# Modulation steps put into VectorE's waits, and two sets of matmul operands made 128 rows high

## The chip, the core and the metric

The kernel runs on one core of one Trainium2 chip. The core has TensorE (PE, with its weight loads PEld), VectorE (DVE), ScalarE (ACT), GpSimd (POOL) and SyncE, whose queue (SP) issues nearly all DMAs. Each engine works through its own queue in the order in which the program was built. The metric is the device time of one execution in microseconds (us); lower is better.

## The reference, cut to what matters

One layer over 512 prompt frames and 64 sample frames, width 2048, all float32:

```python
mod = silu(c) @ w_ada + b_ada                    # 2048 x 12288: sh1, sc1, g1, sh2, sc2, g2
h = rmsnorm(x, norm1) * (1 + sc1) + sh1
proj = h @ w_in                                  # a_q a_k a_v a_r a_lr | b_q b_k b_v b_g b_beta b_alpha
log_a = log_sigmoid(a_lr @ gla_wg + gla_bg) / 16 # GLA's forget gate, rank 16
o_a = GLA recurrence (4 heads);  o_b = gated DeltaNet recurrence (8 heads, short conv on q, k, v)
x = x + g1 * (concat(normed, gated o_a, o_b) @ w_out)
h = rmsnorm(x, norm2) * (1 + sc2) + sh2
x = x + g2 * ConvGLU(h; w_up, conv, w_down)
y = rmsnorm(x, final_norm)
```

The "narrow columns" are the 32 columns of `w_in` for a_lr, b_beta and b_alpha. The "mixers" are the two recurrences.

## The kernel before

**TensorE's big products.** Activations are kept transposed, as 16 tiles of 128 rows by 2 x 288 columns (256 prompt frames and 32 sample frames in each half). Each weight is split on the chip into a rounded part `wh` (ScalarE) and the rest `wl` (VectorE), each activation into `hh` and `hl`, and one weight tile of 128 x 128 takes six matmuls of 288 columns (`mm6`, lines 675 and 677): wh with hh, wh with hl, wl with hh, each for two halves. The stages in order of time: a head (norm, the first 4096 modulation columns, six early columns of `w_in`), the mixer stage (the remaining columns of `w_in`, while the mixers run beside them, then half of the product with `w_out`), the rest of `w_out`, the up projection (seven products in place of eight), the down projection and the final norm.

**The mixer stage and its clock.** After each k-tile of the big products (six matmuls) the program builder runs `tick` (line 632). It moves a modelled time `now` by 0.795 us and asks three kinds of generators for their next piece: tasks (short convolutions, the GLA gate), jobs (`gdn`, `gla`: the mixers) and, last, `ada`. Every VectorE, ScalarE and GpSimd operation of these is recorded through `_Timed` (a wrapper; its operations carry line 2297, and line 2272 where they go with a raised priority), which adds a modelled duration to `free[engine]` and to the generator's own `chain`, the modelled time at which its last result is ready. A mixer yields in `until` as long as `now` has not passed its `chain`. So the order in each queue is that in which these generators were asked, and it is fixed when the program is built.

**Modulation steps.** The other 8192 columns of `silu(c) @ w_ada` are computed on VectorE during the mixer stage, in `ada_blocks` (line 1139): 16 blocks of 512 columns, each 16 k-tiles for two conditions (prompt, sample), 512 steps in all. A step is one `scalar_tensor_tensor` of 128 x 512, `acc = w * c + acc`. Four steps use one loaded tile of 512 KB (`aw` or `xr`, two buffers of each; its load is issued on SP at line 1111, three tiles ahead). Behind each 32 steps `ada_sum` adds the partitions with eight matmuls of 32 rows of output (line 1127), and a task puts the sums into `mod`. Credit `at_ada` grows by 0.72 a tick; in `tick` a step is taken while there is credit and VectorE's modelled backlog `free["V"] - now` is under 1.0 us.

**Who waits for VectorE there.** TensorE, for `wl` of the coming weight tiles (three buffers), for `hl` of the mixers' results ahead of the `w_out` product (`load_o`, line 1516, `hl` at 1523), and for results of the mixers' own steps (`m`, `kt`, `rq`, `sl`, `st` in the rows: scratch, row scales and states of the mixers). GpSimd, in the mixers, does the power -1/2 of norms (`rsqrt`) and two `affine_select` masks per DeltaNet head.

**The operands of the second part.** `narrow` (line 1195) copies the 64 used rows of the narrow columns' product into `na` (64 rows, 576 columns), and sorts them by frame with ten matmuls whose other operand is the selector `sel` (lines 1206 and 1208; each float32 matmul is two records in the profile). `gla_gate` (line 1428) multiplies `na` with `wg`, 64 rows of which 32 hold the gate's weights: one matmul of 512 columns and one of 64 for each of four GLA heads.

Of the kernel before, what the change touches and what calls it, by code (L numbers as in the profile page):

```python
# [8 lines left out]
F32 = mybir.dt.float32  # L9
# [7 lines left out]
P = 128  # L17
D = 2048
KD = 16
TP, TS = 512, 64  # L20

HP, HS, HT = 256, 32, 288
# [9 lines left out]

JOB_RATE, ADA_RATE = 1.0, 0.72
TICK_US, HOP_US, DMA_US, ISSUE_US = 0.795, 0.25, 2.6, 0.5
ADA_BACKLOG, ADA_CREDIT = 1.0, 200.0
OP_US = {"V": (0.12, 1 / 960.0), "A": (0.09, 1 / 1060.0), "G": (0.45, 1 / 400.0)}
TABLE_US, COLUMN_US = 1.28, 0.06
TABLES = {AF.Exp: "exp", AF.Silu: "silu", AF.Ln: "ln"}
# [68 lines left out]
WAIT = "wait"  # L107
# [4 lines left out]
class Kern:  # L112
    def __init__(self, tc, ctx, i, o):
        self.tc, self.nc, self.ctx, self.i, self.o = tc, tc.nc, ctx, i, o
        self.n = 0
        self.cp = ctx.enter_context(tc.tile_pool(name="cp", bufs=1, side="left"))
        self.psum = ctx.enter_context(ExitStack())
        self.pg = self.psum.enter_context(tc.tile_pool(name="pg", bufs=2, space=PSUM))
        self.c, self.scrap = {}, []
        self.now, self.chain, self.free = 0.0, None, dict.fromkeys(OP_US, 0.0)  # L120
        self.table, self.floating, self.last_of = None, False, {}
# [510 lines left out]
    def tick(self):  # L632

        self.now += TICK_US
        self.run_due()
        self.run_tasks(list(self.tasks))
        self.at_job += JOB_RATE
        while self.at_job >= 1:
            self.at_job -= 1
            self.job_step()  # L640
        self.at_ada = min(self.at_ada + ADA_RATE, ADA_CREDIT)
        while self.at_ada >= 1 and self.free["V"] - self.now < ADA_BACKLOG:
            r = next(self.ada, self)
            if r is self or r is WAIT:
                break
            self.at_ada -= 1

    def job_step(self):
        for j in list(self.jobs):
# [545 lines left out]
    def narrow(self, pool):  # L1195

        nc, i, c = self.nc, self.i, self.c
        V, A, T = nc.vector, nc.scalar, nc.tensor
        na = self.na = pool.tile([64, TP + TS], F32, name="na")
        V.tensor_copy(na[:, :TP].rearrange("p (h t) -> p h t", h=2), self.ps_nar[:64, :, :HP])  # L1200
        V.tensor_copy(na[:, TP:].rearrange("p (h t) -> p h t", h=2), self.ps_nar[:64, :, HP:HT])
        self.load_consts(None, NARROW)
        g = lambda n, w=36: pool.tile([P, w], F32, name=n)
        ps = self.bank()
        for b in range(4):
            T.matmul(ps[:, b * 16:(b + 1) * 16], na[:, b * P:(b + 1) * P], c["sel"][:64, :16], start=True, stop=True)
        for h in range(2):
            T.matmul(ps[h * 64:(h + 1) * 64, 64:80], na[:, TP:], c["sel"][:64, :16], start=True, stop=True)
        tmp, at = self.m(), [0]

        def g1(w=36):
# [33 lines left out]
        ps = self.bank()  # L1245
# [6 lines left out]
        ps = self.bank()  # L1252
# [15 lines left out]
        ps = self.bank()  # L1268
# [6 lines left out]
        nc.gpsimd.memset(self.wg, 0.0)  # L1275
        nc.sync.dma_start(self.wg[0:16], i["gla_wg"][0])
        nc.sync.dma_start(self.wg[32:48], i["gla_wg"][0])
# [983 lines left out]
class _Sooner:  # L2261
# [5 lines left out]
    def __getattr__(self, name):  # L2267
        f = getattr(self.engine, name)

        def g(*a, **kw):  # L2270
            with self.tc.high_priority(offset=JOB_AHEAD):
                return f(*a, **kw)  # L2272
        return g


def _size(ap):

    n = 1
    for d in ap.shape[1:]:
        n *= d  # L2280
    return n


class _Timed:
# [5 lines left out]
    def __getattr__(self, name):  # L2290
        f = getattr(self.engine, name)

        def g(*a, **kw):
            out = kw["out"] if "out" in kw else a[0]
            self.k.charge(self.key, _size(out), self.k.action(*a[2:], **kw) if name == "activation" else 0.0)
            with self.k.behind(self.key):
                r = f(*a, **kw)  # L2297
# [96 lines left out]
```

## Time and profile before

| what | value |
|---|---|
| time, median of 3 runs | 2743.76 us (2742.51 to 2744.02) |
| the profiled execution's own time | 2741.56 us |
| its span, from first to last instruction | 2739.9 us |
| granted TensorE clock, mean | 0.999 |
| TensorE busy in the span | 2699.0 us (99%) |
| VectorE busy in the span | 2280.0 us (83%) |

A matmul's end in the profile is modelled and matmuls are pipelined, so TensorE counts as busy also where its stream is only slower. What is lost is better seen in three other places: the time between the starts of two matmul rows, the idle time in brackets of a row with what ended it, and the lists of waits (in total, how often, the longest). In a timeline row stand start, duration, engine, line, operation, output<-inputs, shape, and a count where equal rows were merged. Rows of PEld are the weight loads, one ahead of each matmul.

### The profile page before, as it was taken

How to read it: one execution, taken by the hardware profiler on the slowest of the kernel's cores; microseconds unless marked ns; L12 is line 12 of the kernel's file. 1: busy time of each engine (PE TensorE's matmuls, PEld its weight loads, DVE VectorE, ACT ScalarE, POOL GpSimd, SP SyncE). 2: the span in 40 equal slices, each digit the busy share in tenths (PEclk: the TensorE clock that was granted, in tenths of full speed). 3: DMA queues.
4: the chain of work that ended last, by engine and by line, in shares of the span. 5: the costliest groups of instructions: out<-in, count | busy, mean ns of one | idle time of the engine just before them, and what ended most of it. 6: DMA issues, size and time to landing. Idle time of an engine off the chain costs nothing.

```text
span 2739.9 us, 52447 instructions
## 1 busy us (share of the span) xinstructions
PE 2699.0 (99%) x20404; PEld 2632.7 (96%) x20404; DVE 2280.0 (83%) x3691; ACT 1295.7 (47%) x2286; POOL 473.8 (17%) x440
## 2 busy tenths in 40 slices
PE   7999999999999999999999999999999999999998
PEld 5799999999999989999999999999999999999998
DVE  4578887788888898678999999999999976888896
ACT  4245545545644442454545454545454545333453
POOL 0000100001000000001333333333333300000241
PEclk9999999999999999999999999999999999999999
DMA  9985555555565676534464646455655595664762
GB/s 312 344 266 145 152 154 142 148 145 162 168 170 151 177 240 197 148 101 121 138 191 140 188 144 184 149 181 152 179 152 179 151 316 180 209 217 123 238 179 84
DMA packets 645919, 487.61 MB, mean 178 GB/s; under 512 B 66315, under 2 KB 568070, under 8 KB 645670
## 3 DMA queue, kind: packets, MB, share of 16 engines
q1 hardware_dynamic: 632564, 470.77, 57.5%
q10 hardware_dynamic: 13104, 13.47, 1.7%
q8 instruction: 161, 2.64, 0.4%
q14 instruction: 90, 0.72, 0.1%
HBM read 400.12 MB, written 84.04 MB: 177 GB/s over the span
## 4 chain that ended last, share of the span: by engine, by line
PE 89%; DVE 5%; DMA 3%; ACT 1%; issue 1%; SPq 0%; POOL 0%; ACTq 0%; DVEq 0%
PE g L675 19%; PE bank L1785 17%; PE bank L1784 17%; PE bank L1786 17%; PE g L677 9%; PE bank L2316 5%; PE bank L2312 1%; PE bank L675 1%; DVE acc L2297 1%; DVE m L2272 1%; PE bank L904 1%; PE bank L677 1%; DVE wl L1694 0%; DVE wl L2297 0%; PE g L835 0%
## 5 line engine op out<-in xcount | busy, mean ns | idle before, releaser
L1785 PE MATMUL bank<-slot,wh 128*128 128x290 f32 (+1 forms) x3584 | 1067.3, 298 | 0.0
L1784 PE MATMUL bank<-slot,wh 128*128 128x290 f32 (+1 forms) x3584 | 1063.1, 297 | 1.7 <-DVE v L1807 0.6
L1786 PE MATMUL bank<-slot,wl 128*128 128x290 f32 (+1 forms) x3584 | 1060.0, 296 | 1.7 <-DVE wl L1694 1.7
L1786 PEld LDWEIGHTS bank<-slot,wl 128*128 128x128 f32 x3584 | 680.0, 190 | 3.1 <-DVE wl L1694 2.9
L1784 PEld LDWEIGHTS bank<-slot,wh 128*128 128x128 f32 x3584 | 675.4, 188 | 6.3 <-issue 4.7
L1785 PEld LDWEIGHTS bank<-slot,wh 128*128 128x128 f32 x3584 | 676.9, 189 | 0.1
L675 PE MATMUL g<-hh,wh 128*128 128x288 f32 x2048 | 469.5, 310 | 2.2 <-ACT wh L2297 1.3
L1692 ACT ACTIVATE wh<-raw 128x1024 fp32r<-128x1024 f32 (+1 forms) x304 | 280.7, 924 | 348.2 <-PE bank L1785 323.1
L677 PE MATMUL g<-hh,wl 128*128 128x288 f32 x2048 | 439.4, 296 | 2.4 <-DVE wl L1072 2.1
L675 PE MATMUL g<-hl,wh 128*128 128x288 f32 x2048 | 440.6, 296 | 0.9 <-DVE hl L1523 0.6
L1694 DVE TENSOR_TENSOR wl<-raw,wh 128x1024 fp32r<-128x1024 f32 (+1 forms) x304 | 374.6, 1233 | 69.3 <-ACT wh L1692 66.1
L1692 ACT ACTIVATE wh<-s 128x1024 fp32r<-128x1024 f32 (+1 forms) x228 | 210.9, 927 | 298.2 <-PE bank L1785 139.7
L675 PEld LDWEIGHTS g<-hh,wh 128*128 128x128 f32 x2048 | 323.6, 189 | 18.6 <-issue 11.9
L677 PEld LDWEIGHTS g<-hh,wl 128*128 128x128 f32 x2048 | 328.9, 188 | 4.3 <-DVE wl L1072 2.3
L675 PEld LDWEIGHTS g<-hl,wh 128*128 128x128 f32 x2048 | 328.7, 188 | 3.5 <-issue 1.9
L1694 DVE TENSOR_TENSOR wl<-s,wh 128x1024 fp32r<-128x1024 f32 (+1 forms) x228 | 250.4, 1100 | 14.2 <-ACT wh L1692 12.8
L2297 ACT ACTIVATE wh<-raw 128x1024 fp32r<-128x1024 f32 x135 | 143.3, 1062 | 186.0 <-PE g L675 177.6
L2297 DVE SCALAR_TENSOR_TENSOR acc<-aw,ct,acc 128x512 f32<-128x512 f32 x280 | 198.9, 743 | 2.2 <-DMA aw<-in_w_ada_dram 2.2
L1908 POOL TENSOR_TENSOR j<-j,j 128x288 f32<-128x288 f32 (+1 forms) x120 | 186.1, 1557 | 84.0 <-ACT j L1912 81.8
L2297 DVE TENSOR_TENSOR wl<-raw,wh 128x1024 fp32r<-128x1024 f32 x135 | 166.0, 1230 | 16.9 <-ACT wh L2297 14.3
L2297 DVE SCALAR_TENSOR_TENSOR acc<-xr,ct,acc 128x512 f32<-128x512 f32 x200 | 143.0, 744 | 0.0
L1980 DVE TENSOR_TENSOR slot<-bank,slot 128x288 f32<-128x288 f32 x184 | 83.1, 452 | 34.2 <-PE bank L1786 32.9
(330 smaller groups left out, 3274.2 us busy)
## 6 DMA issues: line engine op xcount, KB each, us to landing
raw<-in_w_up_dram SPq DMA_DIRECT2D x176, 512.0 KB
raw<-in_w_in_dram SPq DMA_DIRECT2D x100, 512.0 KB
raw<-in_w_down_dram SPq DMA_DIRECT2D x128, 320.0 KB
slot<-cd SPq DMA_DIRECT2D x140, 288.0 KB
aw<-in_w_ada_dram SPq DMA_DIRECT2D x78, 512.0 KB
cd<-j SPq DMA_DIRECT2D x120, 288.0 KB
xr<-in_w_ada_dram SPq DMA_DIRECT2D x50, 512.0 KB
hraw<-in_w_ada_dram SPq DMA_DIRECT2D x40, 512.0 KB
```

What stands on the lines that cost most here:

```text
L675: T.matmul(ps[:, h if bank is None else bank, :n], wh, x[:, h, :n], start=f, stop=False)
L677: T.matmul(ps[:, h if bank is None else bank, :n], wl, ah[:, h, :n], start=False, stop=stop)
L904: T.matmul(ps[32 * k:32 * k + 32, :w], cs[:, k0 + k], got[n][k // per][:, k % per], start=(n == together - 1 + 8 * g + 4 * (1 - mi)), stop ...
L1692: self.nc.scalar.activation(hi, src, AF.Copy)
L1694: self.nc.vector.tensor_tensor(lo, src, hi.bitcast(F32), op=ALU.subtract)
L1784: T.matmul(ps, wh[:, j], hi, start=(c < 3 and j == 0), stop=False, skip_group_check=True)
L1785: T.matmul(ps, wh[:, j], lo, start=False, stop=False, skip_group_check=True)
L1786: T.matmul(ps, wl[:, j], hi, start=False, stop=(j == n - 1), skip_group_check=True)
L1908: minus = lambda out, a, b: G.tensor_tensor(out, a, b, op=ALU.subtract)
L1980: V.tensor_tensor(dst, ps, dst, op=ALU.add)
L2297: r = f(*a, **kw)
L2316: return self.engine.matmul(out, *a, **kw)
```

## The change

Two parts that do not depend on each other. First, `_Timed` calls a new function `fill_gap` ahead of every VectorE operation of a mixer or a task. If the operation's `chain` is at least 0.5 us (`GAP_US`) later than the time at which VectorE would be free, modulation steps are taken there, as long as there is credit and that much of a gap. The taking of one step moves into a function of its own, `ada_step`; the taking in `tick` stays. Second, `na` and `wg` get 128 rows, with zeros in the added ones (one more memset on GpSimd, and a taller one), and the matmuls use all 128 rows.

```diff
-ADA_BACKLOG, ADA_CREDIT = 1.0, 200.0
+ADA_BACKLOG, ADA_CREDIT, GAP_US = 1.0, 200.0, 0.5
...
         while self.at_ada >= 1 and self.free["V"] - self.now < ADA_BACKLOG:
-            r = next(self.ada, self)
-            if r is self or r is WAIT:
+            if not self.ada_step():
                 break
-            self.at_ada -= 1
+
+    def ada_step(self):
+        chain, self.chain, self.filling = self.chain, None, True
+        r = next(self.ada, self)
+        self.chain, self.filling = chain, False
+        if r is self or r is WAIT:
+            return False
+        self.at_ada -= 1
+        return True
+
+    def fill_gap(self):
+        if self.filling or self.floating or self.chain is None:
+            return
+        while self.at_ada >= 1 and self.chain - max(self.free["V"], self.now + HOP_US) >= GAP_US:
+            if not self.ada_step():
+                return
...
-        na = self.na = pool.tile([64, TP + TS], F32, name="na")
-        V.tensor_copy(na[:, :TP].rearrange("p (h t) -> p h t", h=2), self.ps_nar[:64, :, :HP])
+        na = self.na = pool.tile([P, TP + TS], F32, name="na")
+        nc.gpsimd.memset(na[64:], 0.0)
+        V.tensor_copy(na[:64, :TP].rearrange("p (h t) -> p h t", h=2), self.ps_nar[:64, :, :HP])
...
-            T.matmul(ps[:, b * 16:(b + 1) * 16], na[:, b * P:(b + 1) * P], c["sel"][:64, :16], start=True, stop=True)
+            T.matmul(ps[:, b * 16:(b + 1) * 16], na[:, b * P:(b + 1) * P], c["sel"][:, :16], start=True, stop=True)
...
-        self.wg = pool.tile([64, 512], F32, name="wg")
+        self.wg = pool.tile([P, 512], F32, name="wg")
...
             out = kw["out"] if "out" in kw else a[0]
+            if self.key == "V":
+                self.k.fill_gap()
             self.k.charge(self.key, _size(out), self.k.action(*a[2:], **kw) if name == "activation" else 0.0)
```

**What moves.** The number of modulation steps, of their loads and of their sums is the same. Their place in VectorE's queue, counted against the weight splits (`wl`) of the stage: at the 60th split 231 of the 512 steps stand ahead before and 265 now, at the 101st, the first tile of `w_out`, 445 and 474; the last step stands ahead of the 114th split before and of the 109th now. Lines below 670 of the kernel before are 16 to 19 higher in the changed one (2272 is 2289, 2297 is 2316, 1523 is 1540).

VectorE, first DeltaNet head, ahead of the memset that opens the 16 x 16 inverses (`m` of 32 rows): the mixer has sent its blocks through DRAM and waits for them; `conv_in` belongs to the next convolution task, `acc` is a modulation step. Before:

```order
L2272 TENSOR_TENSOR m_2702<-bank_2703,m_2355 128x512
L2297 SCALAR_TENSOR_TENSOR acc_2193<-xr_2402,ct,acc_2193 128x512
L2272 TENSOR_TENSOR m_2356<-bank_2716,m_2356 128x512
L2272 TENSOR_TENSOR qkv_2039<-qkv_2039,m_2120 128x512
L2297 SCALAR_TENSOR_TENSOR acc_2194<-xr_2402,ct,acc_2194 128x512
L2297 TENSOR_TENSOR wl_2933<-raw_2931,wh_2932 128x1024
L2297 COPY conv_in<-g_2582 128x64
L2297 COPY conv_in<-cols 128x3
L2272 MEMSET m_2120 32x16
L2272 TENSOR_TENSOR m_2120<-m_2120 32x14 x2
```

Now:

```order
L2316 SCALAR_TENSOR_TENSOR acc_2721<-aw_2628,ct,acc_2721 128x512
L2316 SCALAR_TENSOR_TENSOR acc_2722<-aw_2628,ct,acc_2722 128x512
L2316 SCALAR_TENSOR_TENSOR acc_2721<-aw_2628,ct,acc_2721 128x512
L2316 SCALAR_TENSOR_TENSOR acc_2722<-aw_2628,ct,acc_2722 128x512
L2316 SCALAR_TENSOR_TENSOR acc_2721<-xr_2719,ct,acc_2721 128x512
L2316 SCALAR_TENSOR_TENSOR acc_2722<-xr_2719,ct,acc_2722 128x512
L2316 COPY conv_in<-g_2586 128x64
L2316 COPY conv_in<-cols 128x3
L2316 TENSOR_TENSOR wl_2970<-raw_2968,wh_2969 128x1024
L2316 TENSOR_TENSOR wl_3029<-raw_3027,wh_3028 128x1024
L2289 MEMSET m_2121 32x16
L2289 TENSOR_TENSOR m_2121<-m_2121 32x14 x2
```

The memset stood behind three modulation steps scattered among mixer steps (two of them shown), one weight split and two copies; now thirteen modulation steps in a row, the last six of them shown, two copies and two weight splits stand between the mixer's step before (`qkv`, above the rows shown) and it.

VectorE again, at the first tiles of the `w_out` product, where `load_o` splits eight results of the mixers (`hl`). Before:

```order
L1523 TENSOR_TENSOR hl_12072<-xr_12069,hh_12071 128x576
L1523 TENSOR_TENSOR hl_12078<-raw_12075,hh_12077 128x576
L1523 TENSOR_TENSOR hl_12090<-raw_12087,hh_12089 128x576
L2297 SCALAR_TENSOR_TENSOR acc_11996<-aw_11994,ct,acc_11996 128x512
L2272 COPY_PREDICATED m_11454<-consts_2028,bank_12132 128x2x2x64
L2297 SCALAR_TENSOR_TENSOR acc_11997<-aw_11994,ct,acc_11997 128x512
L2297 SCALAR_TENSOR_TENSOR acc_11996<-aw_11994,ct,acc_11996 128x512
L2297 TENSOR_TENSOR wl_12175<-raw_12173,wh_12174 128x1024
L1523 TENSOR_TENSOR hl_12084<-xr_12081,hh_12083 128x576
L2297 SCALAR_TENSOR_TENSOR acc_11997<-aw_11994,ct,acc_11997 128x512
L2297 TENSOR_TENSOR wl_12253<-raw_12251,wh_12252 128x1024
```

Now:

```order
L1540 TENSOR_TENSOR hl_12116<-raw_12113,hh_12115 128x576
L1540 TENSOR_TENSOR hl_12134<-raw_12131,hh_12133 128x576
L2316 SCALAR_TENSOR_TENSOR acc_11415<-aw_11978,ct,acc_11415 128x512
L2316 SCALAR_TENSOR_TENSOR acc_11416<-aw_11978,ct,acc_11416 128x512
L2316 TENSOR_SCALAR acc_12202<-aw_12059,ct 128x512
L1540 TENSOR_TENSOR hl_12128<-xr_12125,hh_12127 128x576
L1540 TENSOR_TENSOR hl_12146<-raw_12143,hh_12145 128x576
L1540 TENSOR_TENSOR hl_12140<-xr_12137,hh_12139 128x576
L2316 TENSOR_SCALAR acc_12203<-aw_12059,ct 128x512
L2289 TENSOR_TENSOR m_12087<-m_12087,qkv_11347 128x512
L1114 TENSOR_TENSOR mod<-bank_12222,cols 128x4
L2316 TENSOR_TENSOR wl_12244<-raw_12242,wh_12243 128x1024
```

The last `hl` stood behind the split of the second `w_out` tile (`wl_12175`); now all eight stand ahead of it (`wl_12244`). Between the split of the first tile, above the rows shown, and the last `hl` there were 38 rows, now 23.

GpSimd, from the last memset of the head to the first mixer's norm. Before:

```order
L1183 MEMSET nar_1809 128x132
L1275 MEMSET wg 64x512
L2330 AFFINE_SELECT m_2356<-m_2356 128x512
L2330 AFFINE_SELECT m_2355<-m_2355 128x512
L2330 TENSOR_TENSOR kt_2378<-kt_2378,mhalf 128x4
```

Now:

```order
L1199 MEMSET nar_1809 128x132
L1216 MEMSET na 64x576
L1292 MEMSET wg 128x512
L2349 AFFINE_SELECT m_2357<-m_2357 128x512
L2349 AFFINE_SELECT m_2356<-m_2356 128x512
L2349 TENSOR_TENSOR kt_2379<-kt_2379,mhalf 128x4
```

One memset of 64 rows is added ahead of that of `wg`, which is 128 rows high now; nothing else moves there.

More of the change, by code (lines that the diff above doesn't have):

```diff
@@ L120, in __init__ @@
         self.now, self.chain, self.free = 0.0, None, dict.fromkeys(OP_US, 0.0)
-        self.table, self.floating, self.last_of = None, False, {}
+        self.table, self.floating, self.last_of, self.filling = None, False, {}, False
         self.jv, self.ja = _Timed(self, _Sooner(tc, tc.nc.vector), "V"), _Timed(self, _Sooner(tc, tc.nc.scalar), "A")
@@ L1198, in narrow @@
         V, A, T = nc.vector, nc.scalar, nc.tensor
-        na = self.na = pool.tile([64, TP + TS], F32, name="na")
-        V.tensor_copy(na[:, :TP].rearrange("p (h t) -> p h t", h=2), self.ps_nar[:64, :, :HP])
-        V.tensor_copy(na[:, TP:].rearrange("p (h t) -> p h t", h=2), self.ps_nar[:64, :, HP:HT])
+        na = self.na = pool.tile([P, TP + TS], F32, name="na")
+        nc.gpsimd.memset(na[64:], 0.0)
+        V.tensor_copy(na[:64, :TP].rearrange("p (h t) -> p h t", h=2), self.ps_nar[:64, :, :HP])
+        V.tensor_copy(na[:64, TP:].rearrange("p (h t) -> p h t", h=2), self.ps_nar[:64, :, HP:HT])
         self.load_consts(None, NARROW)
@@ L1205, in narrow @@
         for b in range(4):
-            T.matmul(ps[:, b * 16:(b + 1) * 16], na[:, b * P:(b + 1) * P], c["sel"][:64, :16], start=True, stop=True)
+            T.matmul(ps[:, b * 16:(b + 1) * 16], na[:, b * P:(b + 1) * P], c["sel"][:, :16], start=True, stop=True)
         for h in range(2):
-            T.matmul(ps[h * 64:(h + 1) * 64, 64:80], na[:, TP:], c["sel"][:64, :16], start=True, stop=True)
+            T.matmul(ps[h * 64:(h + 1) * 64, 64:80], na[:, TP:], c["sel"][:, :16], start=True, stop=True)
         tmp, at = self.m(), [0]
```

## The prediction, made before the changed kernel had run

> **What bounds the kernel now.** I read the page first, then the busy times of the stretches that the change touches, the lists of waits there, and single places in the timeline.
>
> ```profile
> span 2739.9 us, 52447 instructions
> PE 2699.0 (99%) x20404; PEld 2632.7 (96%) x20404; DVE 2280.0 (83%) x3691; ACT 1295.7 (47%) x2286; POOL 473.8 (17%) x440
> ```
>
> TensorE bounds the whole run; its six matmuls a k-tile are untouched. The change can win only where TensorE waits. The stretches (length, then busy us of each engine; 170 to 1100 is the mixer stage):
>
> ```profile
> core 0: us, PE busy (x) PEld busy (x) DVE busy (x) ACT busy (x) POOL busy (x), PEclk, DMA share, GB/s
> 170.00:950.00 780.00, 778.57 (x6024) 756.67 (x6023) 658.13 (x1422) 408.49 (x974) 64.75 (x52) 1.00 0.58 161
> 950.00:1050.00 100.00, 96.08 (x706) 91.28 (x705) 87.72 (x176) 39.73 (x77) 4.63 (x19) 1.00 0.75 220
> 1050.00:1100.00 50.00, 50.00 (x385) 48.85 (x384) 42.84 (x68) 14.16 (x20) 0.00 (x0) 1.00 0.72 212
> ```
>
> TensorE's idle time is 780 - 778.6 = 1.4 us in the first, 100 - 96.1 = 3.9 in the second, none in the third: 5.3 us in all. That is the pool of the first part. What ended the idle time of the weight loads, from 170 to 950 and then from 950 to 1100 (total, times, longest):
>
> ```profile
> PEld g L675 <- issue: 6.7, 21, 0.4
> PEld g L675 <- PE g L677: 0.7, 1, 0.7
> PEld bank L2316 <- DVE st L2272: 0.6, 1, 0.6
> PEld bank L2316 <- DVE sq L2272: 0.5, 1, 0.5
> ```
>
> ```profile
> PEld g L675 <- ACT wh L2297: 1.6, 1, 1.6
> PEld bank L2316 <- DVE sl L2272: 1.1, 2, 0.7
> PEld bank L2312 <- ACT qkv L2297: 1.0, 1, 1.0
> PEld bank L2312 <- DVE m L2272: 0.9, 1, 0.9
> PEld g L675 <- DVE hl L1523: 0.8, 1, 0.8
> PEld g L677 <- DVE wl L2297: 0.5, 1, 0.5
> ```
>
> The long ones lie late, where the last GLA mixers, the eight `hl` and the first weights of `w_out` meet on a VectorE that is 87.7% busy. "Issue" stands for the 21 times that no producer is named; changes of matmul height or width are among them, and the first part leaves those.
>
> **First part: the moved steps.** A step costs VectorE 0.74 us alone, and four in a row 2.72 us (0.66 apart), before and after; all 512 stay on VectorE.
>
> ```profile
> L2297 DVE SCALAR_TENSOR_TENSOR acc<-aw,ct,acc 128x512 f32<-128x512 f32 x280 | 198.9, 743 | 2.2 <-DMA aw<-in_w_ada_dram 2.2
> 225.62 1.22 DVE L2297 TENSOR_TENSOR wl<-raw,wh 128x1024 fp32r<-128x1024 f32 x1
> 231.25 0.23 DVE L2297 COPY conv_in<-g 128x64 f32<-128x64 f32 x1 [4.41 <-ACT conv_in L2297]
> 280.14 2.72 DVE L2297 SCALAR_TENSOR_TENSOR acc<-aw,ct,acc 128x512 f32<-128x512 f32 x4
> ```
>
> The gap of 4.41 us is the kind that is filled: now thirteen steps stand there, 13 x 0.66 = 8.6 us, so about 4 us of them push `conv_in`, two weight splits and the memset of the inverses back. Neither should show on TensorE: no wait on a weight split stands in the list of 170 to 950, and the inverses' consumers stand further back in TensorE's queue by the same modelled time. By the queue order 29 steps more than before are done ahead of the first `w_out` split, 29 x 0.66 = 19 us of VectorE time taken out of 950 to 1100. That is a share of 19 / 130.6 (87.72 + 42.84) = 15% of its work there, and the `hl` stand closer together. Of the 3.9 us of late idle time I take half as gone, -2.0 us: the waits on `hl`, `wl`, `m` and half of that on `wh` (0.8 + 0.5 + 0.9 + 0.8 = 3.0 of the 5.9 us in that list) have VectorE's queue ahead of them, while `sl` stands behind a DMA of its own (below). The ends are 0 and -3.9.
>
> ```profile
> 1025.15 0.87 DVE L2272 SCALAR_TENSOR_TENSOR sl<-s,s,bank 128x256 f32<-128x256 f32 x2 [1.01 <-DMA out_dram<-sl]
> 1025.68 0.30 PEld L2316 LDWEIGHTS bank<-m,m 128*128 128x128 f32 x2 [0.73 <-DVE sl L2272]
> ```
>
> What is late next: mixer steps from 170 to 950, since VectorE has less slack there: 780 - 658 = 122 us idle, of which the 19 us are taken, 16%. If waits grow as idle time shrinks, 1.4 us becomes 1.7; if the fuller stretch waits like the late one (3.9 in 100 us) on a tenth of its length, +3.0. I take +0.8, nearer to the first, since with the 19 us VectorE is 677 of 780 us busy, 87%, which the late stretch has too, but without the `hl` and the states that meet there; ends -1.4 (all of it goes) and +3.0.
>
> Each moved group of four also issues a 512 KB load on SP, and moves ahead of weight loads queued there.
>
> ```profile
> SPq L1111 <- DVE acc L2297: 221.3, 98, 6.1
> 174.21 5.24 DMA aw<-in_w_ada_dram
> ```
>
> SP already stands 221 us behind modulation tiles that are not yet free, with weight loads (line 777) queued behind, and still only one wait on `wl` reaches TensorE. Freed earlier, a tile is loaded earlier. A run of thirteen steps needs its last tile loaded within 8.6 us of the first step; one landed in 5.24. I put this at nothing; if the cover goes, each of the two longest runs costs VectorE 1 to 3 us, which weight splits made two tiles ahead absorb. The eight summing matmuls of each of the 16 blocks, ScalarE's copy, two transposes and two writes of `mod` move with their block and keep their number: nothing.
>
> **Second part: 128 rows.** One of the four gates, matmul starts; behind it the same engine on float32 operands 128 rows high:
>
> ```profile
> 671.64 0.38 PE L1388 MATMUL bank<-consts,cs 128*72 128x128 f32 x2
> 671.95 1.29 PE L2316 MATMUL bank<-na,wg 64*128 64x512 f32 x4
> 673.17 0.54 PE L675 MATMUL g<-hh,wh 128*128 128x288 f32 x2
> ...
> 218.17 1.05 PE L2316 MATMUL bank<-qkv 128*128 128x128 f32 x8
> 218.97 0.51 PE L675 MATMUL g<-hh,wh 128*128 128x288 f32 x2
> ...
> 1033.76 0.59 PE L2316 MATMUL bank<-sl,m 128*128 128x256 f32 x2
> 1034.19 0.59 PE L2316 MATMUL bank<-m,m 128*128 128x256 f32 x2
> ```
>
> Two records of 128x128 take 0.80 / 4 = 0.20 us, two of 256 columns 0.43. From 671.64 + 0.20 to 673.17 the gate block takes 1.33 us. At 128 rows: 512 columns are 2 x 0.43 = 0.86, the 64-column pair at most 0.20, together 1.06. So -0.27 a gate, -1.1 for four. Ends: 0 (height does not matter) and -0.37 a gate (the pair at 0.10, by its columns), -1.5.
>
> The sorting matmuls, once:
>
> ```profile
> 170.02 0.43 PE L677 MATMUL g<-hh,wl 128*128 128x288 f32 x2
> 170.28 0.43 PE L675 MATMUL g<-hh,wh 128*128 128x288 f32 x2
> 170.64 1.06 PE L1206 MATMUL bank<-consts,na 64*128 64x16 f32 x8
> 171.63 0.29 PE L1208 MATMUL bank<-consts,na 64*64 64x16 f32 x4
> ```
>
> 170.64 to 171.63 is 0.99 for eight; 8 x 0.10 = 0.80 at full height, and the entry of 0.10 goes (170.28 to 170.64 is 0.36, for two matmuls that took 0.26 from 170.02 on); the last four stay 64 wide and keep a change of shape. I take -0.1, ends 0 and -0.3. The added memsets:
>
> ```profile
> 166.58 0.52 POOL L1275 MEMSET wg<- 64x512 f32 x1 [50.70 <-DVE hraw L1091]
> 203.93 1.24 POOL L2330 TENSOR_SCALAR_AFFINE_SELECT m<-m 128x512 f32<-128x512 f32 x2 [36.84 <-DMA m<-gd]
> 280.44 6.49 POOL L2330 TENSOR_SCALAR_AFFINE_SELECT m<-m 128x512 f32<-128x512 f32 x2 [29.05 <-ACT m L2272]
> ```
>
> About 0.5 us for `na` and 0.5 for `wg`, from 166.6 to 167.7, 3 us ahead of the first use at 170.64, and then GpSimd idles until 203.93: nothing. Were that cover gone, the sorting matmuls would wait 0.5 us.
>
> **Sum.** -2.0 + 0.8 - 1.1 - 0.1 = -2.4 us. The profiled execution took 2741.56 us, 1.66 above its span and 2.2 under the median of the runs, so it becomes 2739.2 and the median 2743.76 - 2.4 = 2741.4 us.
>
> **GpSimd in the filled gaps.** The last two rows above are the same pair of masks. VectorE idled beside the first and ran seven modulation steps beside the second:
>
> ```profile
> 206.96 0.23 DVE L2297 COPY conv_in<-g 128x64 f32<-128x64 f32 x1 [4.40 <-ACT conv_in L2297]
> ...
> 282.79 2.06 DVE L2297 SCALAR_TENSOR_TENSOR acc<-xr,ct,acc 128x512 f32<-128x512 f32 x3
> ```
>
> So a mixer's chain grows by 6.49 - 1.24 = 5.25 us where modulation steps fill the wait for a pair of masks, and the modelled clock knows nothing of it. The Trainium skill states a cause (SBUF — State Buffer, section "SBUF: two separate sides"): VectorE and GpSimd share a port pair under an exclusive lock, and a VectorE operation with two SBUF inputs, such as a step, shuts out a GpSimd operation that reads SBUF until it ends. The trace agrees with its 6.49 us; by that rule all masks and norms in filled gaps are late and the sum would be that of the slower rival below, by the lists of waits, which name no GpSimd, it stays -2.4.
>
> **Rivals.**
> *Only redrawn* (25%): the late waits fall on other rows and as many come back, for TensorE works in order and a step displaced by 0.74 us can make a new wait of that size. Then only the second part is left, -1.2 us, or nothing: 2742.6 to 2743.8. For it: the waits named above have nine producers, and none lasts over 1.6 us.
> *All waits go* (16%): -5.3 - 1.2 = -6.5, 2737.3 us. For it: most producers in the lists are VectorE's. Against: `wh`, `qkv` and `sl` do not wait for modulation steps alone.
> *Slower, by GpSimd* (11%): nine pairs of masks, one for each DeltaNet pass, each 5.25 us later, are 47 us of chain, and what is not covered shows on TensorE. At 2.4 us (5%) the gain is eaten, at 7.9 us (17%) it is slower by over 0.2%; a quarter gives +11.8 - 2.4 = +9.4, 2753.2 us. For it: the order puts steps exactly where chains wait. Against: the pair at 280.44 was covered whole, as no wait on GpSimd or a mask stands in the lists.
> That steps do not get ahead at all is excluded by the order itself.
>
> The forecast has 48%, its own range 2740.0 to 2742.8. For 8 in 10 the range reaches into the fast rival and over the redrawn one, and to the ends of the terms: -3.9 - 1.4 - 1.5 - 0.3 = -7.1 gives 2736.7, and +3.0 with nothing gained 2746.8; a little inside these, 2737.0 to 2746.6. A measurement of this kernel can tell 0.2%, 5.5 us, from no change: faster by more has the fast rival's 16%, slower the slower one's 11%, within it are the other 73%.
>
> **What would show it.** After: the gate's rows at 128x512 take about 1.06 us to the next big matmul, and 64-row shapes of `na` are gone; idle TensorE time of 950 to 1050 at 1 to 2.5 us, of 170 to 950 at 1.5 to 3; the last modulation step some 30 us earlier; the masks on GpSimd longer than 1.24 us more often. Wrong it is if TensorE's list names GpSimd or `kt`, `rq`, `s` in whole microseconds (slower), if `wl` appears behind long runs of `acc`, or if the late waits vanish whole (faster).

## The result, and the profile after

The changed kernel is slower: 2749.43 us median of 11 runs (2746.27 to 2751.72) against 2743.83 us for the kernel before beside it (2741.84 to 2747.12), ratio 1.0020, 95% interval 1.0010 to 1.0029. The forecast was 2741.4 us (2737.0 to 2746.6), so it has the wrong sign. The profiled execution took 2750.94 us. First its page's head, then its stretches (length, busy us of each engine, granted clock):

```profile
span 2749.2 us, 52456 instructions
PE 2702.0 (98%) x20404; PEld 2635.1 (96%) x20404; DVE 2281.4 (83%) x3691; ACT 1295.8 (47%) x2286; POOL 468.7 (17%) x441
```

```profile
core 0: us, PE busy (x) PEld busy (x) DVE busy (x) ACT busy (x) POOL busy (x), PEclk, DMA share, GB/s
170.00:950.00 780.00, 772.53 (x5977) 750.94 (x5976) 670.77 (x1444) 405.44 (x968) 61.30 (x52) 1.00 0.59 165
950.00:1050.00 100.00, 95.90 (x696) 90.11 (x695) 85.27 (x177) 43.21 (x81) 4.58 (x19) 1.00 0.69 207
1050.00:1100.00 50.00, 50.00 (x381) 49.23 (x380) 28.09 (x44) 13.32 (x18) 0.00 (x0) 1.00 0.66 181
```

TensorE is idle 780 - 772.5 = 7.5 us from 170 to 950, where it was 1.4, and 4.1 from 950 to 1050, where it was 3.9. VectorE did what the order said: from 950 to 1100 it is busy 85.27 + 28.09 = 113.4 us, 17.2 less than before. TensorE got nothing for it. What TensorE's matmuls waited for (total, times, longest; the longest ones), first in the kernel before from 170 to 950, then in the changed kernel from 170 to 950 and from 950 to 1100:

```profile
PE g L675 <- DVE kt L2297: 0.5, 1, 0.5
PE bank L2316 <- DVE st L2272: 0.4, 1, 0.4
```

```profile
PE bank L2335 <- DVE m L2289: 3.0, 1, 3.0
PE g L691 <- DVE kt L2316: 1.2, 1, 1.2
PE bank L2331 <- ACT m L2289: 1.1, 1, 1.1
PE bank L2335 <- DVE m L2316: 0.8, 1, 0.8
PE bank L1143 <- DVE acc L2316: 0.7, 1, 0.7
```

```profile
PE g L691 <- DVE hl L1540: 1.2, 2, 1.0
PE bank L2335 <- DVE sl L2289: 1.2, 1, 1.2
```

New are long waits on the mixers' own results (`m`, `kt`) and one of `ada_sum` on its own modulation step (`acc`). The longest costs more than it shows. TensorE's rows there, and then three stretches (length, TensorE busy, granted clock, DMA):

```profile
769.49 0.43 PE L693 MATMUL g<-hh,wl 128*128 128x288 f32 x2
772.93 1.19 PE L2335 MATMUL bank<-m 128*128 128x128 f32 x4 [3.01 <-DVE m L2289]
773.77 0.83 PE L691 MATMUL g<-hh,wh 128*128 128x288 f32 x2
...
775.81 0.43 PE L691 MATMUL g<-hl,wh 128*128 128x288 f32 x2
```

```profile
769.50:772.90 3.40, 0.42 (x4) 0.92 0.57 154
772.90:775.80 2.90, 2.87 (x12) 0.51 0.50 124
775.80:778.70 2.90, 2.90 (x23) 1.00 0.11 12
```

Behind the 3.0 us wait the granted clock is one half for 3.4 us (a pair of 288 columns takes 0.83 in place of 0.43), 1.4 us more. So this place costs 4.4 us, not 3.0. The second part did its work: a gate block, counted as the prediction did from 677.62 + 0.20 to 678.84, takes 1.02 us, where it took 1.33, and the sorting 172.92 to 174.04 = 1.12, where 170.64 to 171.85 and an entry of 0.10 were 1.31:

```profile
677.62 0.38 PE L1405 MATMUL bank<-consts,cs 128*72 128x128 f32 x2
677.84 1.19 PE L2335 MATMUL bank<-na,wg 128*128 128x512 f32 x4
678.84 0.51 PE L691 MATMUL g<-hh,wh 128*128 128x288 f32 x2
```

```profile
172.92 0.96 PE L1223 MATMUL bank<-consts,na 128*128 128x16 f32 x8
173.81 0.29 PE L1225 MATMUL bank<-consts,na 128*64 128x16 f32 x4
174.04 0.54 PE L691 MATMUL g<-hl,wh 128*128 128x288 f32 x2
```

**Where the steps went.** At the place of the gap that the prediction quotes as 231.25 (`conv_in`, 4.41 us idle) the changed kernel has, on VectorE and, in the last row, on ScalarE:

```profile
229.60 1.41 DVE L2316 SCALAR_TENSOR_TENSOR acc<-aw,ct,acc 128x512 f32<-128x512 f32 x2
230.93 3.11 DVE L2316 SCALAR_TENSOR_TENSOR acc<-xr,ct,acc 128x512 f32<-128x512 f32 x4
233.97 3.10 DVE L2316 SCALAR_TENSOR_TENSOR acc<-aw,ct,acc 128x512 f32<-128x512 f32 x4
236.99 1.40 DVE L2316 SCALAR_TENSOR_TENSOR acc<-xr,ct,acc 128x512 f32<-128x512 f32 x2
238.32 0.21 DVE L2316 COPY conv_in<-g 128x64 f32<-128x64 f32 x1
```

```profile
234.62 0.65 ACT L2316 ACTIVATE conv_in<-g 128x512 f32<-128x512 f32 x1
```

ScalarE's write ends at 235.27, VectorE's copy starts at 238.32, 3.1 us late. One overshoot that can be followed to TensorE; the rows are VectorE's, ScalarE's and TensorE's:

```profile
365.96 2.72 DVE L2316 SCALAR_TENSOR_TENSOR acc<-xr,ct,acc 128x512 f32<-128x512 f32 x4
368.61 1.39 DVE L2316 SCALAR_TENSOR_TENSOR acc<-aw,ct,acc 128x512 f32<-128x512 f32 x2
369.94 0.20 DVE L2316 COPY conv_in<-g 128x64 f32<-128x64 f32 x1
```

```profile
361.55 0.64 ACT L2316 ACTIVATE conv_in<-g 128x512 f32<-128x512 f32 x1
...
370.31 0.78 ACT L2316 ACTIVATE ca<-conv_in,cols 128x579 f32<-128x579 f32 x1 [3.95 <-DVE kt L2316]
371.00 1.26 ACT L2289 ACTIVATE m<-m,s 128x128 f32<-128x128 f32 x4
```

```profile
371.44 0.62 PE L2331 MATMUL bank<-consts,m 128*128 128x128 f32 x2 [1.13 <-ACT m L2289]
```

Six steps (4.0 us) stand ahead of a copy whose input was ready at 362.19. The copy is 7.75 us late, 4.0 us of it behind the steps and the rest behind rows of the inverses and a weight split, which VectorE was still working on when the input was ready. ScalarE idles 3.95 us for VectorE, its `m` comes late, and TensorE stands 1.13 us.

### The profile page after: what moved, and what is told of

The parts are those of the page before. It is cut to its first block, busy times and chain, and to the rows that moved or that the text cites. A ratio compares the mean times of both kernels' runs of the same rounds, so it can differ in the third digit from the quotient of the medians.

```text
span 2749.2 us, 52456 instructions
## 1 busy us (share of the span) xinstructions
PE 2702.0 (98%) x20404; PEld 2635.1 (96%) x20404; DVE 2281.4 (83%) x3691; ACT 1295.8 (47%) x2286; POOL 468.7 (17%) x441
## 4 chain that ended last, share of the span: by engine, by line
PE 76%; DVE 7%; DMA 2%; ACT 1%; issue 1%; POOL 0%; ACTq 0%; DVEq 0%; SPq 0%; POOLq 0%
PE bank L1802 16%; PE bank L1801 16%; PE bank L1803 16%; PE g L691 14%; PE g L693 7%; PE bank L2335 4%; DVE wl L1711 2%; PE bank L691 1%; DVE m L2289 1%; PE bank L2331 1%; DVE slot L1997 1%; PE bank L693 1%; DVE acc L2316 1%; DVE wl L2316 1%; DVE s L1722 0%
## 5 line engine op out<-in xcount | busy, mean ns | idle before, releaser
L2316 DVE SCALAR_TENSOR_TENSOR acc<-aw,ct,acc 128x512 f32<-128x512 f32 x264 | 188.6, 745 | 2.0 <-DMA aw<-in_w_ada_dram 1.8
L2316 DVE SCALAR_TENSOR_TENSOR acc<-xr,ct,acc 128x512 f32<-128x512 f32 x216 | 153.3, 743 | 0.0
```

## The experiments

Eighteen kernels in five groups, each profiled and timed beside the kernel before. In the table "idle" is TensorE's from 170 to 1100 us by the stretches, "halved" counts stretches of 3.41 us at half clock from 170 to 1130, and "late" is the largest distance from the end of ScalarE's `conv_in` write to the start of VectorE's copy behind it, over the 23 convolutions. The kernel before, timed again in each round, came to medians of 2743.0 to 2744.0 us, so medians of different rounds compare to about 1 us.

| kernel | median us | ratio to before (95%) | idle us | halved | late us |
|---|---|---|---|---|---|
| before (profile) | 2743.8 | 1 | 5.3 | 0 | 3.7 |
| changed kernel, margin 0.5 | 2749.43 | 1.0020 (1.0010 to 1.0029) | 11.6 | 1 | 7.8 |
| rows128 | 2742.03 | 0.9998 (0.9989 to 1.0007) | 5.1 | 0 | 3.7 |
| fill64 | 2748.43 | 1.0020 (1.0011 to 1.0029) | 9.7 | 1 | 7.7 |
| jobs_only | 2741.27 | 0.9993 (0.9984 to 1.0002) | 4.1 | 1 | 3.7 |
| gap1 | 2750.32 | 1.0024 (1.0014 to 1.0034) | 10.2 | 2 | 5.6 |
| gap2 | 2745.17 | 1.0006 (0.9997 to 1.0015) | 6.3 | 1 | 4.0 |
| gap3 | 2741.64 | 0.9992 (0.9984 to 1.0001) | 3.9 | 0 | 3.7 |
| gap4 | 2741.84 | 0.9995 (0.9986 to 1.0004) | 4.5 | 0 | 3.7 |
| fill_dma27 | 2746.68 | 1.0012 (1.0003 to 1.0021) | 8.7 | 0 | 7.7 |
| hold770 | 2747.42 | 1.0016 (1.0007 to 1.0024) | 10.1 | 1 | 7.6 |
| back15 | 2745.07 | 1.0007 (0.9998 to 1.0016) | 6.3 | 1 | 3.7 |
| hop30 | 2747.80 | 1.0018 (1.0009 to 1.0027) | 5.2, and 3.6 at 1114 | 2 | 3.0 |
| dma27 | 2742.63 | 1.0000 (0.9991 to 1.0009) | 4.3 | 0 | 4.4 |
| exponly | 2744.43 | 1.0002 (0.9993 to 1.0011) | 6.4 | 0 | 3.7 |
| expfill | 2753.02 | 1.0032 (1.0020 to 1.0045) | 13.5 | 2 | 6.3 |
| expdma27 | 2751.98 | 1.0029 (1.0018 to 1.0039) | 10.7 | 1 | 6.3 |
| expgap1 | 2745.94 | 1.0010 (1.0002 to 1.0019) | 6.8 | 1 | 6.3 |
| chainonly | 2745.05 | 1.0005 (0.9996 to 1.0014) | 5.6 | 0 | 3.7 |
| chainfill | 2750.09 | 1.0024 (1.0013 to 1.0035) | 6.8 | 2 | 6.4 |

**1. Which part.** rows128 is the second part alone:

```diff
-            if self.key == "V":
-                self.k.fill_gap()
```

> The second part alone: the kernel before with the 128-row operands, no modulation step moved. Theory (the loss of 5.6 us comes from the filled gaps alone): the gates take 1.00 us in place of 1.33 and the sorting 1.12 in place of 1.30, so -1.5 us, about 2742.3, with the idle time of TensorE from 170 to 950 us at the 1.4 us of before. Rival (the taller operands or their memsets cost what the head of the changed profile shows more, +2.3 us to 170 us): 2745 to 2746, and the gates' gain is eaten.

fill64 is the first part alone:

```diff
-        na = self.na = pool.tile([P, TP + TS], F32, name="na")
+        na = self.na = pool.tile([64, TP + TS], F32, name="na")
-        self.wg = pool.tile([P, 512], F32, name="wg")
+        self.wg = pool.tile([64, 512], F32, name="wg")
```

> The first part alone: the changed kernel with operands of 64 rows. Theory (filled gaps cost): 2749.4 + 1.5 = about 2751 us, TensorE idle 7 to 8 us from 170 to 950 and 3 us of it in one place at a mixer's matmul on m, as in the changed kernel. Rival (the taller operands cost, the steps nothing): about 2744.

rows128 came to 2742.03 and fill64 to 2748.43, as the first theory said of rows128, and 2.5 us under what it said of fill64, with the idle time at 5.1 and 9.7 us (5.7 of it from 170 to 950, where 7 to 8 was expected). The loss is the first part's. The gain of rows128 over before, 1.2 us, is inside its interval; the rows of the gates and the sorting show it directly. jobs_only, run later, fills gaps ahead of the mixers' own steps alone:

```diff
-        if self.filling or self.floating or self.chain is None:
+        if self.filling or self.floating or self.chain is None or not self.in_job:
```

> The changed kernel with gaps filled in the mixers' own steps alone, not in the convolutions and gates: the 36 steps ahead of the conv_in copies stay where they were, the ten ahead of the mixers' steps (sample frames, late in the stage) are filled at the margin of 0.5 us. Theory (the fills ahead of conv_in are the loss): 2742 us as with the operands alone, TensorE idle 1.6 us from 170 to 950. Rival (the ten late ones are part of it, for they stand where TensorE's late waits are): 2744 to 2747 and more than 3.5 us idle from 950 to 1050.

2741.27: without the fills ahead of the convolutions and gates the loss is gone, so it is those fills that cost. (In this build six of the ten late steps still find a gap.) No step gets ahead here (231 at the 60th split and 445 at the 101st, as before), so this run alone does not part the fills' place from the lead that they give; section 3 comes back to that. By the builder's clock all the fills that went stand at one place, ahead of the copy `conv_in<-g`, which waits for ScalarE's half of the same tile.

**2. How much of a gap.** That clock, read off while the changed kernel is built, has waits of over 2 us ahead of eight `conv_in` copies; beside them VectorE's idle time just ahead of the same copy in rows128, where nothing fills it:

| modelled wait, us | 5.09 | 8.82 | 4.84 | 3.77 | 8.66 | 9.25 | 4.60 | 4.85 |
|---|---|---|---|---|---|---|---|---|
| idle in rows128, us | 4.20 | 4.41 | 0 | 0 | 3.80 | 5.60 | 0 | 1.63 |
| steps put in, margin 0.5 | 1 | 10 | 7 | 6 | 3 | 0 | 0 | 7 |

The model is 0.9 to 4.9 us too long, seven times of eight more than 3 us. At the three places with 0 VectorE does not wait at all: it is busy with other rows until 0.9 to 2.0 us after ScalarE's write. (Two more of the 36 steps stand at a modelled wait of 1.7 us. Where none went in, a block of 32 steps had just ended, and its generator pauses there for the sum.) So the margin was varied (`GAP_US = 0.5`, here 1.0, 2.0, 3.0 and 4.0):

> GAP_US 1.0 in place of 0.5, both parts. Theory 1 (the modelled wait ahead of the conv_in copies is 3.2 to 4.6 us longer than the real one, and what overshoots it is the loss): a margin of 1.0 us still overshoots by 2 to 4 us, conv_in copies 3 us or more behind ScalarE's write at several places, 2746 to 2749 us. Theory 2 (only draws of the order): no relation to the margin, anything from 2741 to 2749.

> GAP_US 2.0 in place of 0.5, both parts: steps are taken only while 2 us of the modelled wait are left, so each filled gap keeps 1.35 to 2 us idle. By the order of the queue as many steps get ahead (285 of 512 at the 60th weight split, 265 in the changed kernel). Theory (the filled gaps took the idle time that covered work which the modelled clock puts too early, by a microsecond or two): most of the cover is back, TensorE idle 2 to 3 us from 170 to 950, 2743 to 2745 us. Rival 1 (steps ahead cost by themselves, through their loads on the queue of the weights or through VectorE's share): 2749 or more. Rival 2 (it is only a draw: any other order lets waits fall elsewhere): anything from 2740 to 2752 with idle time that follows no margin.

> GAP_US 3.0, both parts. Theory 1: an overshoot of 1.5 us at most, 2742 to 2744 us, between the 2745.2 of a margin of 2.0 and the 2741.8 of 4.0. Theory 2 (draws): anything from 2741 to 2749.

> GAP_US 4.0 in place of 0.5, both parts. Ahead of the conv_in copies the modelled wait of the changed kernel was 1.7 to 9.3 us, while VectorE idled there 0 to 5.6 us in the kernel with the operands alone, mostly 3.5 to 4.5 us less. With a margin of 4.0 us the steps put into a gap should fit the real wait. Theory 1 (the modelled wait is too long, and what overshoots it is the loss): no conv_in copy comes more than 1 us after ScalarE's conv_in write, where the changed kernel had 5.6 and 7.8 us, TensorE idle 1.5 to 2.5 us from 170 to 950, and 2741 to 2743 us. Theory 2 (getting steps ahead, or any new order, costs some 3 us here whatever the margin, as with a margin of 2.0 and with the larger backlog): 2744 to 2747.

2750.3, 2745.2, 2741.6 and 2741.8: the loss falls with the margin and is gone at 3.0, about where it should be by the table above. gap1 is 1.3 us above what was expected, gap3 0.4 under. (Late copies of 3.7 us are there without any fill, so the mark of 1 us set for gap4 was too strict.) The gap at 231.25 as gap4 fills it:

```profile
229.38 2.73 DVE L2316 SCALAR_TENSOR_TENSOR acc<-xr,ct,acc 128x512 f32<-128x512 f32 x4
232.03 1.41 DVE L2316 SCALAR_TENSOR_TENSOR acc<-aw,ct,acc 128x512 f32<-128x512 f32 x2
233.82 0.22 DVE L2316 COPY conv_in<-g 128x64 f32<-128x64 f32 x1 [0.39 <-ACT conv_in L2316]
```

```profile
170.00:950.00 780.00, 777.48 (x6023) 756.17 (x6023) 674.00 (x1448) 409.28 (x974) 84.65 (x53) 1.00 0.59 164
950.00:1050.00 100.00, 98.03 (x722) 92.56 (x721) 86.04 (x176) 42.55 (x81) 4.66 (x19) 1.00 0.75 224
```

The steps fill the wait and 0.39 us are left. TensorE's late idle time is 2.0 us, its early one 2.5: what the prediction had forecast of the change itself (1.9 and 2.2) comes out where the steps fit. Neither gap3 nor gap4 can be told from rows128 or from the kernel before by their intervals, so there is no version here that is shown to beat both.

**3. Getting ahead, or any other order.** back15 gets the steps as far ahead without a filled gap (`ADA_BACKLOG` 1.0 to 1.5, operands of 128 rows):

> The kernel before with the 128-row operands and ADA_BACKLOG 1.5 in place of 1.0: no gap is filled, but tick takes a step while VectorE's modelled backlog is under 1.5 us. The steps get ahead as far as in the changed kernel or further (270 of 512 at the 60th split, 503 at the 101st, 474 in the changed kernel). Theory (the place in the waits costs, not getting ahead): idle 1.4 to 3 us from 170 to 950, less than 3.9 from 950 to 1050, 2740 to 2743 us. Rival 1 (getting ahead costs by itself): 2747 to 2751. Rival 2 (a draw): anything from 2740 to 2752.

hop30 and dma27 redraw the order with nothing ahead (`HOP_US` 0.25 to 0.30; `DMA_US` 2.6 to 2.7, both on rows128), fill_dma27 redraws the changed kernel in the same way:

> A redraw for its own sake: the kernel with the 128-row operands alone, HOP_US 0.30 in place of 0.25, so that the generators are asked at slightly other modelled times. Nothing gets ahead (233 of 512 steps at the 60th split, 231 before; 433 at the 101st, 445 before). Theory 1 (the loss is that of filled gaps and of steps ahead): 2742 us as with the operands alone, within 1.5 us. Theory 2 (the order of before is a lucky one, and any other meets a new long wait somewhere): 2744 to 2747 us, with one wait over 1.7 us and a halved clock in the mixer stage.

> A second redraw: the kernel with the 128-row operands alone, DMA_US 2.7 in place of 2.6. Nothing gets ahead (235 of 512 steps at the 60th split, 439 at the 101st). Theory 1 (the loss is that of filled gaps and of steps ahead): 2742 us, within 1.5 us. Theory 2 (any other order meets a new long wait somewhere): 2744 to 2747 us, with one wait over 1.7 us and a halved clock in the mixer stage.

> The changed kernel (margin 0.5, both parts) redrawn by DMA_US 2.7, which by itself moved the kernel with the operands alone by only 0.6 us (2742.6). Theory 1 (the overshoot is the loss, whatever the draw): 2746 to 2750 us, conv_in copies 3 us or more late again, TensorE idle 4 us or more from 170 to 950. Theory 2 (the 2749.4 was an unlucky draw): 2742 to 2745 us.

hop30 fell against the first theory: 2747.8 with no step ahead. Its profile shows why, a wait of 2.8 us for a `wh` at 1001 and one of 3.1 us at 1117, just where the second half of `w_out` begins, each with its halved clock:

```profile
1114.12 0.44 PE L693 MATMUL g<-hh,wl 128*128 128x288 f32 x2
1117.66 0.80 PE L691 MATMUL g<-slot,wh 128*128 128x288 f32 x4 [3.10 <-ACT wh L2314]
```

```profile
1114.50:1117.60 3.10, 0.06 (x1) 1.00 1.21 293
1117.60:1121.90 4.30, 3.78 (x16) 0.62 1.21 290
```

So a redraw by itself can cost 5 us, and dma27, exponly, chainonly and back15 (2742.6 to 2745.1) show that it often costs 0 to 3. A single slower kernel proves little here. But with the fills at a margin of 0.5, all three draws under the clock as it was (changed kernel, fill_dma27, hold770) came to 2746.7 to 2749.4, and fill_dma27 lost 4.0 us to dma27 by the medians (3.0 by each one's distance to its own before) with neither the 3.0 us wait nor a halved stretch: the waits of 1.2, 0.7 and 1.1 us at 210, 225 and 371 are in it again, of which only the last was followed to an overshoot above. Getting ahead by itself is not the changed kernel's loss: gap3 has more steps ahead at the 60th split (271, 265) and loses nothing. A bigger lead is another matter: the five kernels with 281 to 304 steps there (gap1, gap2, expfill, expdma27, chainfill) lie 1.9 to 9.4 us over their own before, and no run parts that lead from their fills.

**4. The longest wait.** hold770 takes no step in `tick` while the inverses near 770 are recorded:

```diff
-        while self.at_ada >= 1 and self.free["V"] - self.now < ADA_BACKLOG:
+        while self.at_ada >= 1 and self.free["V"] - self.now < ADA_BACKLOG and not HOLD[0] < self.now < HOLD[1]:
```

> The changed kernel, but tick takes no modulation step while the modelled clock is between 564 and 590 us, the stretch in which the ninth set of inverses is recorded (seven steps stand just ahead of it in the changed kernel). Theory (the longest wait of the changed kernel, 3.0 us on m at 770 us, comes from those steps, and the halved clock of 3.4 us that follows it is its consequence): the wait and the halved clock both go, -3.0 - 1.4, about 2745 us. Rival (VectorE's queue stands there behind a weight split that waits 2.5 us for ScalarE, whatever the steps do): the wait stays at 2 us or more and the time at 2748 to 2750.

2747.4, 2.0 us less where 4.4 was expected (1.1 by each one's distance to its own before). The wait of 3.0 us and its halved clock went, and another came in the late stretch, with a halved clock of its own:

```profile
PE bank L2332 <- ACT qkv L2317: 3.4, 1, 3.4
```

```profile
955.00:958.80 3.80, 0.38 (x4) 0.15 (x2) 1.55 (x6) 1.03 (x4) 0.00 (x0) 1.00 0.13 41
958.80:962.80 4.00, 4.00 (x20) 3.92 (x21) 2.75 (x8) 0.99 (x4) 0.00 (x0) 0.57 0.06 12
```

No filled gap stands at 770, only steps that `tick` took, and fill_dma27, with the same fills ahead of `conv_in`, has no such wait. That it belongs to the draw and not to the fills is likely, then, but argued and not shown.

**5. Why the model is long, and whether mending it helps.** In the DeltaNet mixer a third exponential on ScalarE is recorded behind two GpSimd masks that it does not need. The builder's clock adds the masks (2 x 1.73 = 3.46 us) to the mixer's `chain`, and ScalarE's next work, `conv_in` with it, is modelled behind that; on the chip ScalarE goes on at once. The first edit moves the exponential ahead of the masks (exponly without fills, expfill and expdma27 at a margin of 0.5, expgap1 at 1.0):

```diff
         A.activation(du, du, AF.Exp, scale=-1.0)
+        A.activation(gb, gb, AF.Exp)
...
-        A.activation(gb, gb, AF.Exp)
```

> No gap filled, operands of 128 rows; in the DeltaNet mixer the third exponential (gb) is recorded ahead of the two masks in place of behind them. ScalarE and GpSimd get the same instructions in the same order; only the modelled clock changes. A control: 2742 us within 1.5 by every theory that blames the filled gaps.

> The changed kernel (gaps filled to 0.5 us) with the third exponential recorded ahead of the two masks. Theory 1 (the modelled gap was 3.46 us too long because the masks were counted into ScalarE's queue, and the overshoot is the loss): gaps now end where ScalarE's conv_in write ends, no conv_in copy more than 1.5 us behind it (5.6 and 7.8 us in the changed kernel), TensorE idle 1.5 to 3 us from 170 to 950, 2741 to 2744 us, though as many steps stand ahead as before (288 of 512 at the 60th split). Theory 2 (a margin of 0.5 is too small by itself, or getting ahead costs): 2746 to 2750.

> The same as the changed kernel with the exponential recorded first, redrawn by DMA_US 2.7. Theory 1: 2741 to 2744 us again, against 2746.7 of the same redraw with the exponential behind the masks. Theory 2: 2746 to 2750.

> GAP_US 1.0 with the exponential recorded first. Theory 1: 2741 to 2744 us, against 2750.3 at the same margin with the exponential behind the masks. Theory 2: 2746 to 2750.

This edit misses its aim: ScalarE's following squares take over the `chain` with the masks in it, and most modelled waits stay at 5.0 to 8.8 us (up to 13 steps put in). So these are three more draws of the overshoot: late copies of 6.3 us, 2753.0 and 2752.0, and 2745.9 at the wider margin, against 2744.4 without fills. (2745.9 is between the two theories' ranges, and 1.5 us is within what a redraw moves.) The second edit keeps the masks out of the chain (chainonly without fills, chainfill at a margin of 0.5):

```diff
+        end = self.chain
         self.pool.affine_select(du, du, ...)
...
+        self.chain = end
         A.activation(gb, gb, AF.Exp)
```

> Operands of 128 rows, no gap filled; the modelled time of the two GpSimd masks (2 x 1.73 us) no longer counts into the mixer's chain, so ScalarE's following instructions are modelled 3.46 us earlier. The control of chainfill; by itself a redraw with more steps ahead (262 of 512 at the 60th split), 2741 to 2746 us.

> The changed kernel, margin 0.5, with the masks kept out of the chain. The modelled waits ahead of conv_in become 0.9 to 2.2 us (1.7 to 8.8 in the changed kernel), so 1 to 3 steps go into one where 10 went. Theory 1 (the loss is the overshoot of gaps modelled too long): no conv_in copy more than 2 us behind ScalarE's write, and within 1.5 us of chainonly, 2742 to 2746 us, although more steps stand ahead than in any kernel so far (304 at the 60th split). Theory 2 (a margin of 0.5, or so many steps ahead, cost by themselves): 2747 to 2753.

Now the modelled waits are 0.9 to 2.2 us and one to three steps go into one, yet chainfill takes 2750.1, 5 us more than chainonly. That is theory 2's number, and theory 1 does not explain it. One copy is still 6.4 us late, but behind the inverses' own rows, two steps and a weight split, not behind a burst of steps; in the profiled executions a wait of 2.0 us at 1026 draws two halved stretches (3.2 us), idle time is 1.2 us more than in chainonly, and some 5 us of the mixer stage lie in small delays that neither holds. A clock that is right about the masks alone doesn't make a margin of 0.5 safe. chainfill also has the largest lead of all, 304 steps at the 60th split and all 512 at the 101st, so the lead may be what costs here; no run tells.

**What is shown, and what is open.** Shown: the loss is the fills ahead of `conv_in` (jobs_only), it shrinks with the margin and is gone at 3.0 (gap1 to gap4), and a late VectorE copy reaches TensorE (371.44, 1.13 us). Argued from the margins, and followed at that one place only: that the overshoot is how the fills cost. Over all kernels the late copy goes with the loss: the nine with one over 5 us took 2745.9 to 2753.0, of the eleven others ten 2741.3 to 2745.2, and hop30 2747.8. Open: what chainfill loses 5 us to, whether a large lead costs by itself, and why this order is so much more sensitive than the model's error alone would have it.

## Why the prediction was wrong, point by point

*The pushed work (the step that failed).* The prediction saw it: 13 steps of 0.66 us in a gap of 4.41, some 4 us pushed back, and then said "Neither should show on TensorE ... the inverses' consumers stand further back in TensorE's queue by the same modelled time." That step failed: the modelled time it leaned on ran 0.9 to 4.9 us beyond the real gap at the places that were filled, so TensorE's queue was set by a clock on which VectorE was not late. What TensorE showed in place of nothing were waits of 3.0, 1.2 and 0.8 us on VectorE's `m` and `kt`, of 1.1 us on ScalarE's `m`, and of 0.7 us on `acc`; how much of them is overshoot stays open, but for the 1.1. The term +0.8 (ends -1.4 and +3.0) measured +6.0 by idle time from 170 to 950, and its upper end was too low as well.

*The price of a wait.* The sum counted a wait at its length. The halved clock behind it made the longest one 1.4 us dearer, a cost that no term held. Idle time and halved clock over those of rows128, 6.5 + 1.4 = 7.9 us, are about the 7.4 us between the two medians (6.8 by each one's distance to its own before).

*The late idle time.* The 17.2 us of VectorE work went out of 950 to 1100 as worked out (19), but the term -2.0 came out as +0.2: waits on `hl` and `sl` came back in other places. Where the fills fit, the term was near (3.9 to 2.0 in gap4, to 2.8 in gap3).

*Second part.* Gates -0.31 each against -0.27, sorting -0.2 against -0.1, memsets nothing: right, about -1.4 us in all.

*Queue of loads.* Costed at nothing, and no wait on `aw`, `xr` or `wl` in whole microseconds appeared: right.

*The rivals.* "Slower, by GpSimd" had the sign, and its 2753.2 is 3.8 us over what came, but it had not the cause. The nine pairs of masks took 1.2 to 3.3 us here, none 6.49, and its own mark, GpSimd in TensorE's list, is absent. The pair in the filled gap at 231.25 and the longest one of the changed kernel, and behind them the two longest of gap4:

```profile
232.27 2.27 POOL L2349 TENSOR_SCALAR_AFFINE_SELECT m<-m 128x512 f32<-128x512 f32 x2 [6.75 <-ACT m L2289]
...
428.23 3.28 POOL L2349 TENSOR_SCALAR_AFFINE_SELECT m<-m 128x512 f32<-128x512 f32 x2 [39.95 <-ACT m L2289]
```

```profile
491.77 11.65 POOL L2349 TENSOR_SCALAR_AFFINE_SELECT m<-m 128x512 f32<-128x512 f32 x2 [34.67 <-ACT m L2289]
...
556.23 13.29 POOL L2349 TENSOR_SCALAR_AFFINE_SELECT m<-m 128x512 f32<-128x512 f32 x2 [32.86 <-ACT m L2289]
```

gap4 decides it: there two pairs, beside VectorE rows without a pause, take 11.65 and 13.29 us, 10 to 12 us over the 1.24 of a pair alone and more than the 5.25 us that the rival gave each of nine; GpSimd is busier than in the changed kernel (84.65 us from 170 to 950, against 61.30), and nothing is lost. So the effect is real, and it was covered. "Only redrawn" named a real effect, but priced a new wait at 0.74 us, where redraws cost up to 5. `kt` in whole microseconds, named as a mark of "slower", did appear.

*The base.* The profiled execution of before lay 2.2 us under the median of its runs. It has no halved stretch in the head, like dma27's; all other profiles have one or two there, at up to 1.7 us each.

## What to carry to other kernels

A gap that a modelled clock shows is to be filled only as far as the clock's error leaves room: compare modelled waits with the idle times in the trace first, and keep that difference as the margin. On an engine that works in order, what overshoots delays everything behind it, also work of chains that were not waiting. And where many orders are possible, redraw the kernel once or twice without the change before its loss or gain is believed, because a new order alone moved this one by up to 5 us.

## What the runs showed of the hardware

TensorE's clock is halved in fixed slots. In 20 profiles every stretch at half clock before the run's end is one slot of 3.41 us (two in a row twice), and within a run they start at whole multiples of 3.413 us from each other (after 215 slots in the changed kernel). Taking slots on that grid from 20 us on, all 24 in which TensorE was busy less than 0.445 of the time were followed by a slot at half clock, of some 40 with 0.445 to 0.56 busy 15 were, and above that two (0.68 and 0.86 busy, the second itself at half clock). One from the head of rows128, busy 1.62 of 3.41 us:

```profile
100.75:104.16 3.41, 1.62 (x12) 1.00 1.07 400
104.16:107.57 3.41, 3.41 (x17) 0.50 1.10 373
```

In this kernel, then, a wait under (1 - 0.56) x 3.41 = 1.5 us cost itself; one of more than (1 - 0.445) x 3.41 = 1.9 us, where it fell into one slot, cost up to half a slot, 1.7 us, besides (1.4 at 772.3, where TensorE still idled 0.6 us of the slot); and where it lies on the grid is a matter of chance, one source of the scatter between runs. The Trainium skill (TensorE: Matmul & The Clock Gate, section "Part 1: The HAM clock gate (the "warmup" mystery)") has the free-running window of 3413 ns and the half rate, which these traces bear out, but names a whole idle window of about 3.4 us as the cause; here half of one was enough.

A modulation step also slows beside GpSimd's masks: four took 3.11 us from 230.93 on, with masks running from 232.27, against 2.72 at 365.96. The masks lose more: beside the pair of 13.29 us in gap4 VectorE ran steps, weight splits and rows of a convolution without a pause, where a pair beside an idle VectorE took 1.24.
